# Gate and up of a SwiGLU FFN by seven block products in six of eleven pairs

## The chip, the core and the metric

The kernel runs on one NeuronCore of a Trainium2 chip. The metric is the device time of one execution in microseconds (us). TensorE (PE) multiplies, VectorE (DVE), ScalarE (ACT) and GpSimd (POOL) do the elementwise work, and the queue of SyncE (SP) issues most loads from memory (DMA). Every engine works through its own instruction stream and waits for others at semaphores. Products land in PSUM, eight banks of 128 x 512 float32; all else lies in SBUF.

## What is computed

One layer of a decoder trunk: 512 tokens of width 1024 in float32. A norm, an input projection, a gated-MLP group beside a sparse-attention group, an output projection and a residual; then the part that changes, an FFN of inner width 2816, and a last norm:

```python
h = rmsnorm(x, norm_ffn_w[l])
x = x + (jax.nn.silu(h @ w_gate[l]) * (h @ w_up[l])) @ w_down[l]
return rmsnorm(x, final_norm_w)
```

## The kernel before

Precision is held by splitting. Every operand of a product is split into a high part in fp32r (a copy on ScalarE, `copy_a`, L79) and a low part, the float32 remainder (a subtraction on VectorE, `sub`, L76). `mm3` (L113) then makes three products of one: high by high, high by low, low by high. Products of the trace at L114, L115 and L116 are these three.

The FFN starts behind `ffn_norm`, which turns the normed tokens by transposes (against the tile `ident`) and keeps them as `h2h` and `h2l`, each two tiles of 4 contraction blocks x 512 tokens. The inner width is 22 blocks of 128 columns, in 11 pairs. `gate_up(f)` (L720) loads the gate and the up columns of one block (512 KB each, `load_raw`, L85, three buffers "wr"), splits them into half-weight buffers ("wh", eight of 4 KB a partition) and multiplies: for gate and for up 8 contraction blocks by `mm3`, 512 tokens wide, which is 48 products into two PSUM banks. Block 0 is done in two halves of 256 tokens, because its second half waits for the last norm. `gate_act(f)` (L696) applies SiLU on ScalarE and the multiplication by up on VectorE; after the second block of a pair it also forms four sums of token and width quarters (`ss`) and splits all seven pieces into `ah` and `al`.

`down` (L782) is already a product by seven: it takes a group of pairs (`FFN_GROUPS`: 2, 3, 3 and 3 pairs), loads 1 MB of down weights a pair ("wd", three buffers of their own), and makes seven products M1, M2, M5, M6, M3, M7, M4. For each it splits one quarter or one combination of quarters of every pair's weights (`product`, L789); the combinations are formed in place in the raw buffer (`diffs`, `t2_of`, `t4_of`, L808 to L816), so a raw buffer comes free only when M4's weights have been split. The results are added into the residual `x2` (`accumulate`, L774), mostly twice each.

The program is written in this order: block by block, then the group's `down`, then the next group. The scheduler of the tile framework sets the order within each engine's stream when the program is built: it places what is ready by a timing model of its own, earlier program text first, so splits of later weights stand between earlier work where buffers allow. A tile waits for a free buffer of its tag. Pools that were closed (`first_pools`) leave their place to the pools of the FFN (`weights_f`, `temps_f`, L763), and a new tile waits for the old tiles that lay there.

Of the kernel before, what the change touches and what calls it, by code (L numbers as in the profile page):

```python
# [18 lines left out]
P = 128  # L19
S = 512  # L20
# [11 lines left out]
NG = 24  # L32
FFN_GROUPS = (4, 6, 6, 6)
START = (("S", 0), ("T", 0), ("W", 0), ("K", 0), ("S", 1), ("T", 1), ("W", 1), ("S", 2), ("K", 1), ("T", 2),
         ("W", 2), ("S", 3), ("K", 2), ("T", 3), ("W", 3), ("K", 3))
BANKS = (3, 2, 2, 1)
NBIG, NP, NRAW, NSPL, T4, T2 = 11, 3, 3, 4, 3, 4
NHALF, NDOWN = 8, 3


@with_exitstack
def hybrid_gmlp_nsa_kernel(
# [16 lines left out]
    wp, tp, sp = [p.__enter__() for p in first_pools]  # L59

# [28 lines left out]

    def split(raw, shape, name, eng=None, spare=False, behind=None, halves=False):  # L90
        if spare:
            w = bp.tile([P, 2, *shape], F32R, tag="P", name=f"{name}_s", bufs=NP)
            hi, lo = w[:, 0], w[:, 1]
        elif halves:
            hi = wp.tile([P, *shape], F32R, tag="wh", name=f"{name}_h", bufs=NHALF)
            lo = wp.tile([P, *shape], F32R, tag="wh", name=f"{name}_l", bufs=NHALF)
# [8 lines left out]
    def load_cols(w, r0, nk, c0, n, name, eng=None, spare=False, behind=None, halves=False):  # L105
        src = w[r0:r0 + nk * P, c0:c0 + n].rearrange("(k p) f -> p k f", p=P)
        return split(load_raw(src, [nk, n], name), [nk, n], name, eng, spare, behind, halves)

# [9 lines left out]
    def bcast_row(vec, n, name, tag=None):  # L118
        t = cp.tile([P, DM if tag else n], F32, name=name, tag=tag or name)[:, :n]
        nc.sync.dma_start(t, bass.AP(tensor=vec.tensor, offset=vec.offset, ap=[[0, P], [1, n]]))  # L120
        return t
# [18 lines left out]

    ident = cp.tile([P, P], F32, name="ident")
    make_identity(nc, ident)
    ones = cp.tile([1, P], F32, name="ones")
    nc.vector.memset(ones, 1.0)
# [48 lines left out]
    ps = zp.__enter__()  # L193
    NB = {**dict(zip("MSTO", BANKS)), "G": 2, "A": 2, "B": 2, "C": 2}

# [76 lines left out]
    maskw = cp.tile([P, S], F32, name="maskw")  # L272
# [3 lines left out]
    cmask = cp.tile([P, NT, 32], F32, name="cmask")  # L276
# [3 lines left out]
    valid = cp.tile([P, 1], F32, name="valid")  # L280
    nc.gpsimd.memset(valid, 1.0)
# [4 lines left out]
    nc.tensor.transpose(vps[:, :80], vec, ident[:80, :80])  # L286
    vecT = cp.tile([P, 80], F32, name="vecT")
    copy_a(vecT, vps[:, :80])
# [37 lines left out]

    sel = cp.tile([2 * NX, NX], F32, name="sel")
    done = nc.vector.tensor_tensor(out=sel, in0=ident[:2 * NX, 0:NX], in1=ident[:2 * NX, NX:2 * NX], op=OP.add)
    after(done, kept)
    pair = cp.tile([P, 2, 32], F32, name="pair")  # L330
# [129 lines left out]
    for k in range(4):  # L460
        pt = bank("T", [P, NT, P], f"pta{k}")
        for t in range(NT):
# [223 lines left out]
    acts = []  # L686
    n_act = [0]
    raw_act = [None]

    def act_tile(name):  # L690
        n_act[0] += 1
        if (n_act[0] - 1) % 8 < NP:
            return bp.tile([P, 7, 256], F32R, tag="P", name=name, bufs=NP)
        return b8([P, 7, 256], F32R, name)

    def gate_act(f):  # L696
        pg, e = gu.pop(f)[1], f % 2
        if e == 0:
            raw_act[0] = t4([P, 4, 256], F32, f"sg{f}")
        sg = raw_act[0]  # L700
        own = sg[:, 2 * e:2 * e + 2].rearrange("p a c -> p (a c)")
        nc.scalar.activation(own, pg[0], AF.Silu)
        nc.vector.tensor_tensor(out=own, in0=pg[1], in1=own, op=OP.mult)  # L703
        if e == 0:
            return
        ss = t4([P, 4, 256], F32, f"ss{f}")
        ah, al = act_tile(f"ah{f}"), act_tile(f"al{f}")
# [7 lines left out]
        acts.append((ah, al))  # L715


    gu = {}

    def gate_up(f, part=None):  # L720
        if not part:
            behind = mixed[-1] if f == 0 else last_norm if f == 1 else None
            ws = [load_cols(w, 0, KD, f * P, P, f"w{'gu'[a]}{f}", spare=f == 0, behind=behind, halves=f > 0)
                  for a, w in ((0, w_gate), (1, w_up))]
            gu[f] = ws, [bank("G" if part is None else "S", [P, S], f"gu{f}{a}") for a in range(2)]
        cut = slice(0, S) if part is None else slice(part * 256, part * 256 + 256)
# [55 lines left out]
    def down(gi, pairs):  # L782
        raws = []
        for p in pairs:
            r = wp.tile([P, 2, 2, 512], F32, tag="wd", name=f"wd{p}_r", bufs=NDOWN)
            nc.sync.dma_start(r, w_down[2 * p * P:(2 * p + 2) * P].rearrange("(e p) (h c) -> p e h c", p=P, h=2))
            raws.append(r)

        def product(name, slot, tag, first, src, before=None):  # L789
# [51 lines left out]

    f0 = 0
    onw = None
    for gi, nb in enumerate(FFN_GROUPS):
        acts.clear()
        for f in range(f0, f0 + nb):
            if f > 0:
                gate_up(f)
                gate_act(f)
# [53 lines left out]
```

## Time and profile before

| what | value |
|---|---|
| median of three runs | 619.64 us (615.88 to 620.91) |
| the profiled execution | 617.18 us |
| its span, first to last instruction | 615.4 us |
| granted TensorE clock, mean | 0.998 |
| bytes moved by DMA | 61.33 MB, mean 100 GB/s |

The rows further down name the engine, the line of the kernel, the operation and the tiles it writes and reads, with partitions x elements. On a timeline row the first number is the start from the beginning of the span, the second the duration, both in us; a bracket tells how long the engine stood idle before it and what ended that. Successive instructions of one engine overlap in part, so the distance of two starts is what one costs in a run of them, not its duration.

### The profile page before, as it was taken

Reading aid. Unit: us, or ns where it says so; the run is one execution under the profiler, and the core shown is the slowest. Engines: PE = TensorE matmul, PEld = TensorE weight load, DVE = VectorE, ACT = ScalarE, POOL = GpSimd, SP = SyncE. Lnnn points to the kernel's source line nnn. Section 1 sums busy time; section 2 is a strip of 40 time slices with the busy share of each in tenths; the row PEclk is TensorE's granted clock in tenths of the full one; section 3 lists DMA queues with packets and bytes.
Section 4 is the critical chain, followed back from the end, with each engine's and each line's share of the span. In section 5 each row is a group of like instructions: output and inputs, shape, how many; then the busy total and the mean of one; then the engine's idle time right before and its main releaser. Section 6 shows DMA issues by size and latency. Waiting matters only on the chain.

```text
span 615.4 us, 7662 instructions
## 1 busy us (share of the span) xinstructions
PE 598.2 (97%) x2812; PEld 487.3 (79%) x2812; DVE 400.7 (65%) x729; ACT 297.7 (48%) x547; POOL 68.2 (11%) x113
## 2 busy tenths in 40 slices
PE   8999899998999999999999999999999999999994
PEld 5878778786788777888888888888888888888883
DVE  4752779647898976746694437794437694446696
ACT  6653367649877875434342323442323353233354
POOL 3100100004453473000000000000000000000001
PEclk9999999999999999999999999999999999999999
DMA  8451534534000012089036331037321028320003
GB/s 292 147 143 50 180 114 143 175 123 143 2 2 1 1 36 68 1 240 304 4 98 210 103 103 34 1 138 238 99 87 56 1 96 260 89 68 1 0 2 136
DMA packets 73495, 61.33 MB, mean 100 GB/s; under 512 B 3681, under 2 KB 64113, under 8 KB 73458
## 3 DMA queue, kind: packets, MB, share of 16 engines
q1 hardware_dynamic: 72880, 59.80, 31.4%
q10 hardware_dynamic: 578, 1.05, 0.5%
q8 instruction: 22, 0.36, 0.3%
q14 instruction: 15, 0.12, 0.1%
HBM read 58.74 MB, written 2.10 MB: 99 GB/s over the span
## 4 chain that ended last, share of the span: by engine, by line
PE 87%; DVE 5%; DMA 2%; POOL 2%; ACT 2%; issue 1%; POOLq 0%; SPq 0%; DVEq 0%; ACTq 0%
PE gu L115 13%; PE gu L116 13%; PE gu L114 13%; PE o L652 3%; PE pA L114 3%; PE ptp L632 3%; PE pA L115 3%; PE pA L116 3%; PE s L558 3%; PE po L115 2%; PE po L116 2%; PE po L114 2%; PE pC L114 2%; PE pC L115 2%; PE pC L116 2%
## 5 line engine op out<-in xcount | busy, mean ns | idle before, releaser
L114 PE MATMUL gu<-h2h,wg_h 128*128 128x512 f32 x168 | 65.4, 389 | 0.0
L115 PE MATMUL gu<-h2l,wg_h 128*128 128x512 f32 x168 | 65.4, 389 | 0.0
L116 PE MATMUL gu<-h2h,wg_l 128*128 128x512 f32 x168 | 65.4, 389 | 0.0
L114 PE MATMUL gu<-h2h,wu_h 128*128 128x512 f32 x168 | 65.4, 389 | 0.0
L115 PE MATMUL gu<-h2l,wu_h 128*128 128x512 f32 x168 | 65.4, 389 | 0.0
L116 PE MATMUL gu<-h2h,wu_l 128*128 128x512 f32 x168 | 65.4, 389 | 0.0
L79 ACT ACTIVATE wu_h<-wu_r 128x1024 fp32r<-128x1024 f32 x21 | 22.3, 1061 | 64.9 <-PE gu L115 48.4
L703 DVE TENSOR_TENSOR sg<-gu,sg 128x512 f32<-128x512 f32 x22 | 15.2, 692 | 57.0 <-PE gu L116 57.0
L76 DVE TENSOR_TENSOR wg_l<-wg_r,wg_h 128x1024 fp32r<-128x1024 f32 x21 | 25.7, 1223 | 40.7 <-ACT wg_h L79 40.3
L79 ACT ACTIVATE wg_h<-wg_r 128x1024 fp32r<-128x1024 f32 x21 | 22.3, 1060 | 47.8 <-PE gu L115 40.9
L169 POOL TENSOR_TENSOR rstd_y<-s_y,mhalf 128x1 f32<-128x1 f32 x4 | 3.0, 754 | 345.9 <-DVE s_y L166 341.1
L563 ACT ACTIVATE P<-P,nm 128x128 f32<-128x128 f32 (+3 forms) x64 | 35.5, 559 | 5.4 <-DVE nm L561 5.1
L82 POOL TENSOR_SCALAR P<-P,sm 128x128 f32<-128x128 f32 (+3 forms) x64 | 34.1, 556 | 32.2 <-DVE sm L570 15.0
L116 PEld LDWEIGHTS gu<-h2h,wu_l 128*128 128x128 f32 x168 | 31.6, 188 | 6.6
L116 PEld LDWEIGHTS gu<-h2h,wg_l 128*128 128x128 f32 x168 | 31.5, 187 | 6.6
L114 PEld LDWEIGHTS gu<-h2h,wg_h 128*128 128x128 f32 x168 | 31.6, 188 | 6.5
L115 PEld LDWEIGHTS gu<-h2l,wu_h 128*128 128x128 f32 x168 | 31.5, 188 | 6.6
L115 PEld LDWEIGHTS gu<-h2l,wg_h 128*128 128x128 f32 x168 | 31.5, 188 | 6.5
L114 PEld LDWEIGHTS gu<-h2h,wu_h 128*128 128x128 f32 x168 | 31.5, 188 | 6.5
L561 DVE CUSTOM_DVE_ANT_0 P<-s,maskw 128x128 f32<-128x128 f32 (+3 forms) x64 | 29.5, 481 | 4.5 <-PE s L558 4.0
L652 PE MATMUL o<-PT,Vt 128*128 128x512 f32 x80 | 31.1, 439 | 0.2
L76 DVE TENSOR_TENSOR PT<-ptp,PT 128x512 fp32r<-128x512 f32 x40 | 26.6, 684 | 5.7 <-ACT PT L79 5.5
(510 smaller groups left out, 1501.6 us busy)
## 6 DMA issues: line engine op xcount, KB each, us to landing
wg_r<-in_w_gate_dram SPq DMA_DIRECT2D x22, 512.0 KB, 4.7
wu_r<-in_w_up_dram SPq DMA_DIRECT2D x22, 512.0 KB, 3.9
wd_r<-in_w_down_dram SPq DMA_DIRECT2D x11, 1024.0 KB, 4.8
wo_r<-in_w_o_dram SPq DMA_DIRECT2D x8, 512.0 KB, 4.8
x_sb<-in_x_dram SPq DMA_DIRECT2D x4, 512.0 KB, 8.3
wv_r<-in_w_in_dram SPq DMA_DIRECT2D x4, 512.0 KB, 6.7
wu_r<-in_w_in_dram SPq DMA_DIRECT2D x4, 512.0 KB, 5.0
w1k_r<-in_cmp_k_w_dram SPq DMA_DIRECT2D x4, 512.0 KB, 4.3
```

The lines of the kernel that those rows point to most:

```text
L76: return (eng or nc.vector).tensor_tensor(out=o, in0=a, in1=hi.bitcast(F32), op=OP.subtract)
L79: return nc.scalar.activation(o, a, AF.Copy)
L82: nc.gpsimd.tensor_scalar(out=o, in0=a, scalar1=s, scalar2=1.0, op0=OP.mult, op1=OP.mult)
L114: nc.tensor.matmul(ps, lhsT=sh, rhs=mh, start=first, stop=False, skip_group_check=more)
L115: nc.tensor.matmul(ps, lhsT=sh, rhs=ml, start=False, stop=False, skip_group_check=more)
L116: nc.tensor.matmul(ps, lhsT=sl, rhs=mh, start=False, stop=last, skip_group_check=more)
L558: nc.tensor.matmul(sb, lhsT=q, rhs=KAB[kv][:, a, b0:b0 + nbr, :n], start=(a == 0), stop=(a == 1))
L561: nc.vector.tensor_tensor_reduce(out=pr, in0=sb[:, br], in1=maskw[:, S - n:], scale=-0.125, scalar=BIG, op0=OP.add, op1=OP.min, accum_out= ...
L563: e = nc.scalar.activation(pr, pr, AF.Exp, bias=nm[b], scale=-1.0, accum_out=sm[b])
L632: nc.tensor.transpose(pt[:, hh], src, ident)
L652: nc.tensor.matmul(of, lhsT=Vt[:, b0 + br, j, kv], rhs=PTs[u][:, a], start=(first and a == 0), stop=False)
L703: nc.vector.tensor_tensor(out=own, in0=pg[1], in1=own, op=OP.mult)
```

## The change

For the pairs 2, 3, 5, 6, 8 and 9 gate and up are computed together as a 2 x 2 block product by seven products in place of eight: the rows of the result are gate and up, the contraction is halved, the tokens are halved. So the products are 256 tokens wide, and weights and tokens are combined beforehand: the token combinations once (`token_sums`), the weight combinations in each pair, in place. The other pairs are done plainly but loaded and split by pair. The sums of the seven products are finished on VectorE and ScalarE in the buffers `sg` and `ss`.

The raw buffers are pooled anew: one tag "wr" of three 1 MB buffers serves gate, up and down loads. The constants of the first part (`ident` among them) move from the lasting pool to one of the pools that are closed before the FFN, ahead of the others there. PSUM has six banks of one tag and two for "B". The activations `ah`, `al` lie in named places (`ACT_HOMES`), with two buffers "xa" in the weights pool. The diff, cut:

```diff
-FFN_GROUPS = (4, 6, 6, 6)
+FFN_GROUPS = (2, 3, 3, 3)
+SEVEN = (2, 3, 5, 6, 8, 9)
+ACT_HOMES = (("xa", "xa", "b8", "P"), ("P", "P", "P", "b8", "xa", "xa"))
...
-NHALF, NDOWN = 8, 3
+NHALF, NPAIR, NXA = 8, 3, 2
...
-    first_pools = [tc.tile_pool(name="weights", bufs=2), tc.tile_pool(name="temps", bufs=3),
+    first_pools = [tc.tile_pool(name="consts_a", bufs=1), tc.tile_pool(name="weights", bufs=2), tc.tile_pool(name="temps", bufs=3),
...
-    ident = cp.tile([P, P], F32, name="ident")
+    ident = kp.tile([P, P], F32, name="ident")
...
-    NB = {**dict(zip("MSTO", BANKS)), "G": 2, "A": 2, "B": 2, "C": 2}
+    NB = {**dict(zip("MSTO", BANKS)), "G": 6, "B": 2}
...
+    def keep_acts(p, sg, ss):
+        ah, al = act_tile(f"ah{p}"), act_tile(f"al{p}")
         copy_a(ah[:, 0:3], sg[:, 1:4])
...
+        elif part is None:
+            raw = wp.tile([P, 2, KD, P], F32, tag="wr", name=f"wgu{f}_r", bufs=NPAIR)
+            ws = []
+            for a, w in ((0, w_gate), (1, w_up)):
+                nc.sync.dma_start(raw[:, a], w[:, f * P:(f + 1) * P].rearrange("(k p) f -> p k f", p=P))
+                ws.append(halves(raw[:, a], [KD, P], f"w{'gu'[a]}{f}", last_norm))
...
+    def halves(src, shape, name, behind=None):
+        hi, lo = [wp.tile([P, *shape], F32R, tag="wh", name=f"{name}_{c}", bufs=NHALF) for c in "hl"]
+        for step in (copy_a(hi, src), sub(lo, src, hi)):
...
+    def pair_raw(p):
+        raws = []
+        for c, w in (("g", w_gate), ("u", w_up)):
+            r = wp.tile([P, KD, 256], F32, tag="wr", name=f"w{c}{p}_r", bufs=NPAIR)
+            nc.sync.dma_start(r, w[:, p * 256:(p + 1) * 256].rearrange("(k p) f -> p k f", p=P))
+            raws.append(r)
+        return raws
+
+    def plain_pair(p):
+        sg, ss = t4([P, 4, 256], F32, f"sg{p}"), t4([P, 4, 256], F32, f"ss{p}")
+        z = {}
+        for a, r in enumerate(pair_raw(p)):
+            for kh in range(2):
+                hi, lo = halves(r[:, 4 * kh:4 * kh + 4], [4, 256], f"w{'gu'[a]}{p}{kh}")
+                for e in range(2):
+                    if kh == 0:
+                        z[e, a] = bank("G", [P, S], f"gu{p}{a}{e}")
+                    for k in range(4):
+                        c = slice(e * P, (e + 1) * P)
+                        mm3(z[e, a], hi[:, k, c], lo[:, k, c], h2h[kh][:, k], h2l[kh][:, k],
+                            kh + k == 0, kh == 1 and k == 3)
+        for e in range(2):
+            gate_act(sg, e, (z[e, 0], z[e, 1]))
+        keep_acts(p, sg, ss)
...
+    def token_sums():
+        rs = []
+        for a in range(2):
+            r = bp.tile([P, 2, 4, 256], F32, tag="P", name=f"tok{a}", bufs=NP)
+            for c in range(2):
+                cut = slice(c * 256, c * 256 + 256)
+                nc.vector.tensor_tensor(out=r[:, c], in0=h2h[a][:, :, cut].bitcast(F32),
+                                        in1=h2l[a][:, :, cut].bitcast(F32), op=OP.add)
+            rs.append(r)
+        y11, y12, y21, y22 = rs[0][:, 0], rs[0][:, 1], rs[1][:, 0], rs[1][:, 1]
+        for o, x, y in ((y11, y12, y11), (y12, y22, y12), (y22, y22, y11), (y21, y21, y22)):
+            nc.vector.tensor_tensor(out=o, in0=x, in1=y, op=OP.subtract)
+        for a in range(2):
+            hi, lo = b8([P, 2, 4, 256], F32R, f"th{a}"), b8([P, 2, 4, 256], F32R, f"tl{a}")
+            for c in range(2):
+                copy_a(hi[:, c], rs[a][:, c])
+                sub(lo[:, c], rs[a][:, c], hi[:, c])
...
+    def seven_pair(p):
+        sg, ss = t4([P, 4, 256], F32, f"sg{p}"), t4([P, 4, 256], F32, f"ss{p}")
+        sgv = sg.rearrange("p (e a) c -> p e a c", a=2)
+        gate, late, up2 = sgv[:, :, 0], sgv[:, :, 1], ss[:, 0:2]
+        rg, ru = pair_raw(p)
+        a11, a12, a21, a22 = rg[:, 0:4], rg[:, 4:8], ru[:, 0:4], ru[:, 4:8]
...
+            for e in range(2):
+                c = slice(e * P, (e + 1) * P)
+                for k in range(4):
+                    mm3(z[tag][:, e], w[0][:, k, c], w[1][:, k, c], y[0][:, k], y[1][:, k],
+                        first and e + k == 0, k == 3, not first or e > 0)
...
+        w = unit(1, a11)
+        vec2(a11, a11, a21, OP.subtract)
+        vec2(a21, a21, a22, OP.add)
+        product(1, "A", w, y11)
+        copy_a(gate, z["A"])
+        w = unit(5, a21)
+        vec2(a21, a22, a11, OP.subtract)
+        product(5, "C", w, t1)
+        copy_a(up2, z["C"])
+        product(6, "A", unit(6, a21), t2n)
+        copy_a(late, z["A"])
+        w = unit(2, a12)
+        vec2(a12, a12, a21, OP.subtract)
+        product(2, "B", w, y21)
+        vec2(gate, z["B"], gate, OP.add)
+        nc.scalar.activation(gate, gate, AF.Silu)
+        product(7, "A", unit(7, a11), t3)
+        vec2(up2, z["A"], up2, OP.add)
+        product(3, "C", unit(3, a12), y22)
+        vec2(late, z["C"], late, OP.add)
+        nc.scalar.activation(late, late, AF.Silu)
+        product(4, "A", unit(4, a22), t4n)
+        vec2(gate, z["A"], gate, OP.mult)
+        vec2(late, up2, late, OP.mult)
+        keep_acts(p, sg, ss)
...
-            r = wp.tile([P, 2, 2, 512], F32, tag="wd", name=f"wd{p}_r", bufs=NDOWN)
+            r = wp.tile([P, 2, 2, 512], F32, tag="wr", name=f"wd{p}_r", bufs=NPAIR)
...
+        for p in range(p0, p0 + n):
+            if p == 0:
+                gate_act(sg0, 1, gate_up(1))
+                keep_acts(0, sg0, ss0)
+            elif p in SEVEN:
+                seven_pair(p)
+            else:
+                plain_pair(p)
+        if gi == 0:
+            token_sums()
```

## Rows read from the trace of the kernel before

**Rows 1.** The page, part 1: busy time, share of the span, instructions
```profile
PE 598.2 (97%) x2812; PEld 487.3 (79%) x2812; DVE 400.7 (65%) x729; ACT 297.7 (48%) x547; POOL 68.2 (11%) x113
```

**Rows 2.** Busy time by engine in four stretches of the FFN
```profile
core 0: us, PE busy (x) PEld busy (x) DVE busy (x) ACT busy (x) POOL busy (x), PEclk, DMA share, GB/s
273.00:283.90 10.90, 10.90 (x51) 9.04 (x50) 5.84 (x6) 4.74 (x6) 0.00 (x0) 1.00 0.96 308
283.90:305.75 21.85, 21.85 (x98) 18.07 (x97) 14.77 (x21) 7.33 (x12) 0.00 (x0) 1.00 0.39 126
305.75:325.70 19.95, 19.95 (x88) 16.25 (x87) 18.89 (x28) 9.93 (x14) 0.00 (x0) 1.00 0.37 127
390.30:419.10 28.80, 28.80 (x127) 23.57 (x126) 26.88 (x41) 14.42 (x21) 0.00 (x0) 1.00 0.32 107
```

**Rows 3.** Timeline of PE: start us, duration us, line, what it computes
```profile
270.20 0.28 PE L116 MATMUL gu<-h2h,wg_s 128*128 128x256 f32 x1
...
273.08 0.40 PE L114 MATMUL gu<-h2h,wg_h 128*128 128x512 f32 x1
...
283.99 0.39 PE L114 MATMUL gu<-h2h,wg_h 128*128 128x512 f32 x1
...
305.75 0.39 PE L114 MATMUL pA<-wd0M,ah 128*128 128x512 f32 x1
```

**Rows 4.** Timeline of DVE around 310 us
```profile
308.10 0.42 DVE L711 TENSOR_TENSOR ss<-ss,sg 128x256 f32<-128x256 f32 x1
308.43 0.95 DVE L76 TENSOR_TENSOR al<-sg,ah 128x768 fp32r<-128x768 f32 x1
309.30 0.42 DVE L711 TENSOR_TENSOR ss<-sg,ss 128x256 f32<-128x256 f32 x1
309.63 0.68 DVE L76 TENSOR_TENSOR wd0M<-wd_r,wd0M 128x512 fp32r<-128x512 f32 x1
310.24 0.68 DVE L776 TENSOR_TENSOR x<-pA,x 128x512 f32<-128x512 f32 x1
310.84 1.22 DVE L76 TENSOR_TENSOR al<-ss,ah 128x1024 fp32r<-128x1024 f32 x1
311.99 0.68 DVE L776 TENSOR_TENSOR x<-pA,x 128x512 f32<-128x512 f32 x1
```

**Rows 5.** Timeline of ACT, same stretch
```profile
309.75 1.06 ACT L79 ACTIVATE ah<-ss 128x1024 fp32r<-128x1024 f32 x1 [1.62 <-DVE ss L711]
310.72 0.61 ACT L79 ACTIVATE wd1M<-wd_r 128x512 fp32r<-128x512 f32 x1
```

**Rows 6.** Timeline of SP's queue, then PE, at the second down group
```profile
408.38 3.01 SPq L786 DMA_DIRECT2D wd_r<-in_w_down_dram  x2
...
411.03 0.37 SPq L786 DMA_DIRECT2D wd_r<-in_w_down_dram  x1
...
390.31 0.39 PE L114 MATMUL pA<-wd2M,ah 128*128 128x512 f32 x1
...
419.10 0.39 PE L114 MATMUL gu<-h2h,wg_h 128*128 128x512 f32 x1
```

**Rows 7.** The page, part 6: DMA issues of 1 MB, count, KB each, us to landing
```profile
wd_r<-in_w_down_dram SPq DMA_DIRECT2D x11, 1024.0 KB, 4.8
```

**Rows 8.** Timeline of all engines at the start of the FFN
```profile
264.01 0.38 SPq L87 DMA_DIRECT2D wg_r<-in_w_gate_dram  x1
...
265.10 3.33 SPq L87 DMA_DIRECT2D wg_r<-in_w_gate_dram  x1
...
265.47 1.04 PE L180 MATMUL pt_f<-ident,xf 128*128 128x128 f32 x8
...
270.27 1.06 ACT L79 ACTIVATE wg_h<-wg_r 128x1024 fp32r<-128x1024 f32 x1 [3.08 <-DMA wg_r<-in_w_gate_dram]
```

**Rows 9.** Waits in 300 to 600 us: total us, times, longest
```profile
engine line waited for: us in total, times, longest us
DVE sg L703 <- PE gu L116: 54.5, 19, 3.4
```

More of the change, by code (lines that the diff above doesn't have):

```diff
@@ L56, in hybrid_gmlp_nsa_kernel @@
     bp = ctx.enter_context(tc.tile_pool(name="big", bufs=NBIG))
-    first_pools = [tc.tile_pool(name="weights", bufs=2), tc.tile_pool(name="temps", bufs=3),
+    first_pools = [tc.tile_pool(name="consts_a", bufs=1), tc.tile_pool(name="weights", bufs=2), tc.tile_pool(name="temps", bufs=3),
                    tc.tile_pool(name="small", bufs=4)]
-    wp, tp, sp = [p.__enter__() for p in first_pools]
+    kp, wp, tp, sp = [p.__enter__() for p in first_pools]
     def b8(shape, dt, name):
@@ L88, in load_raw, with split @@
         return raw
-    def split(raw, shape, name, eng=None, spare=False, behind=None, halves=False):
+    def split(raw, shape, name, eng=None, spare=False, behind=None):
         if spare:
@@ L103, in split, with load_cols @@
         return hi, lo
-    def load_cols(w, r0, nk, c0, n, name, eng=None, spare=False, behind=None, halves=False):
+    def load_cols(w, r0, nk, c0, n, name, eng=None, spare=False, behind=None):
         src = w[r0:r0 + nk * P, c0:c0 + n].rearrange("(k p) f -> p k f", p=P)
-        return split(load_raw(src, [nk, n], name), [nk, n], name, eng, spare, behind, halves)
+        return split(load_raw(src, [nk, n], name), [nk, n], name, eng, spare, behind)
     def after(later, earlier):
@@ L118, in bcast_row @@
     def bcast_row(vec, n, name, tag=None):
-        t = cp.tile([P, DM if tag else n], F32, name=name, tag=tag or name)[:, :n]
+        t = (cp if tag else kp).tile([P, DM if tag else n], F32, name=name, tag=tag or name)[:, :n]
         nc.sync.dma_start(t, bass.AP(tensor=vec.tensor, offset=vec.offset, ap=[[0, P], [1, n]]))
@@ L286, in hybrid_gmlp_nsa_kernel @@
     nc.tensor.transpose(vps[:, :80], vec, ident[:80, :80])
-    vecT = cp.tile([P, 80], F32, name="vecT")
+    vecT = kp.tile([P, 80], F32, name="vecT")
     copy_a(vecT, vps[:, :80])
@@ L324, in blocks @@
         sub(X2[nm][:, :, 1, :], xff, X2[nm][:, :, 0, :])
-    sel = cp.tile([2 * NX, NX], F32, name="sel")
+    sel = kp.tile([2 * NX, NX], F32, name="sel")
     done = nc.vector.tensor_tensor(out=sel, in0=ident[:2 * NX, 0:NX], in1=ident[:2 * NX, NX:2 * NX], op=OP.add)
     after(done, kept)
-    pair = cp.tile([P, 2, 32], F32, name="pair")
+    pair = kp.tile([P, 2, 32], F32, name="pair")
     idv = ident.rearrange("p (a e n) -> p a e n", a=2, e=2)
@@ L686, in hybrid_gmlp_nsa_kernel @@
     acts = []
-    n_act = [0]
-    raw_act = [None]
+    homes = []
     def act_tile(name):
[L691 to L707, printed above, removed]
+        tag = homes.pop(0)
+        if tag == "b8":
+            return b8([P, 7, 256], F32R, name)
+        pool, n = (bp, NP) if tag == "P" else (wp, NXA)
+        return pool.tile([P, 7, 256], F32R, tag=tag, name=name, bufs=n)
+    def keep_acts(p, sg, ss):
+        ah, al = act_tile(f"ah{p}"), act_tile(f"al{p}")
         copy_a(ah[:, 0:3], sg[:, 1:4])
@@ L715, in gate_act @@
         acts.append((ah, al))
+    def gate_act(sg, e, pg):
+        own = sg[:, 2 * e:2 * e + 2].rearrange("p a c -> p (a c)")
+        nc.scalar.activation(own, pg[0], AF.Silu)
+        nc.vector.tensor_tensor(out=own, in0=pg[1], in1=own, op=OP.mult)
     gu = {}
     def gate_up(f, part=None):
-        if not part:
-            behind = mixed[-1] if f == 0 else last_norm if f == 1 else None
-            ws = [load_cols(w, 0, KD, f * P, P, f"w{'gu'[a]}{f}", spare=f == 0, behind=behind, halves=f > 0)
+        if part == 0:
+            ws = [load_cols(w, 0, KD, f * P, P, f"w{'gu'[a]}{f}", spare=True, behind=mixed[-1])
                   for a, w in ((0, w_gate), (1, w_up))]
-            gu[f] = ws, [bank("G" if part is None else "S", [P, S], f"gu{f}{a}") for a in range(2)]
+            gu[f] = ws, [bank("S", [P, S], f"gu{f}{a}") for a in range(2)]
+        elif part is None:
[4 more added lines that the diff above has]
+                ws.append(halves(raw[:, a], [KD, P], f"w{'gu'[a]}{f}", last_norm))
+            gu[f] = ws, [bank("G", [P, S], f"gu{f}{a}") for a in range(2)]
         cut = slice(0, S) if part is None else slice(part * 256, part * 256 + 256)
@@ L730, in gate_up @@
                     k == 0, k == KD - 1)
+        return gu[f][1]
+    def halves(src, shape, name, behind=None):
+        hi, lo = [wp.tile([P, *shape], F32R, tag="wh", name=f"{name}_{c}", bufs=NHALF) for c in "hl"]
+        for step in (copy_a(hi, src), sub(lo, src, hi)):
+            if behind is not None:
+                after(step, behind)
+        return hi, lo
+    def pair_raw(p):
[5 more added lines that the diff above has]
+        return raws
@@ new lines, in hybrid_gmlp_nsa_kernel @@
+    TH, TL = [], []
+    def token_sums():
[15 more added lines that the diff above has]
+                sub(lo[:, c], rs[a][:, c], hi[:, c])
+            TH.append(hi)
+            TL.append(lo)
@@ new lines, in seven_pair, with vec2, product, unit @@
+    def seven_pair(p):
[4 more added lines that the diff above has]
+        a11, a12, a21, a22 = rg[:, 0:4], rg[:, 4:8], ru[:, 0:4], ru[:, 4:8]
+        t1, t3, t4n, t2n = [(TH[a][:, c], TL[a][:, c]) for a in range(2) for c in range(2)]
+        y11, y21, y22 = [(h2h[a][:, :, c], h2l[a][:, :, c])
+                         for a, c in ((0, slice(0, 256)), (1, slice(0, 256)), (1, slice(256, 512)))]
+        z = {}
+        def vec2(o, x, y, op):
+            nc.vector.tensor_tensor(out=o, in0=x, in1=y, op=op)
+        def product(n, tag, w, y):
+            first = tag not in z
+            if first:
+                z[tag] = bank("G", [P, 2, 256], f"g{tag}{p}")
+            for e in range(2):
[3 more added lines that the diff above has]
+                        first and e + k == 0, k == 3, not first or e > 0)
+        def unit(n, src):
+            return halves(src, [4, 256], f"w{p}M{n}")
+        w = unit(1, a11)
[23 more added lines that the diff above has]
+        keep_acts(p, sg, ss)
@@ L800, in product @@
                 if first:
-                    banks[tag, c] = bank(tag, [P, 512], f"p{tag}{gi}{c}")
+                    banks[tag, c] = bank("B" if tag == "B" else "G", [P, 512], f"p{tag}{gi}{c}")
                 z, ts = banks[tag, c], slice(c * P, (c + 1) * P)
@@ L840, in down @@
             add(0, 0, "A")
-    f0 = 0
+    p0 = 0
     onw = None
-    for gi, nb in enumerate(FFN_GROUPS):
+    for gi, n in enumerate(FFN_GROUPS):
         acts.clear()
[L846 to L849, printed above, removed]
+        homes[:] = ACT_HOMES[min(gi, 1)]
+        for p in range(p0, p0 + n):
[8 more added lines that the diff above has]
+            token_sums()
         if gi == len(FFN_GROUPS) - 1:
             onw = bcast_row(final_norm_w, DM, "onw", tag="wb")
-        down(gi, range(f0 // 2, (f0 + nb) // 2))
-        f0 += nb
+        down(gi, range(p0, p0 + n))
+        p0 += n
     def finish(t, order):
```

28 lines of the change are left out of this document (13 added, 15 removed).

## The prediction

> **What bounds the kernel now.** I read the page's table of engines first: TensorE is busy 97% of the span, VectorE 65%, ScalarE 48% [rows 1]. [...] So from 273 us to the end of the products the time is the number of products times their spacing, and VectorE, which splits every weight into a high and a low part, is next in line. Then the timeline of PE for that spacing, since a product's own duration (0.28 or 0.39 us) overlaps with its neighbours: 24 products of 256 columns start between 270.20 and 273.08 us, 0.120 us each; the 96 of 512 columns of one pair take 283.99 to 305.75 us, 21.76 us or 0.2267 us each [rows 3]. Half the columns cost 53%, not 50%.
>
> **TensorE.** A plain pair is 2 blocks x 2 matrices x 8 contraction tiles x 3 terms = 96 products of 512 columns: 21.76 us. A pair by seven products is 7 x 2 blocks x 4 tiles x 3 terms = 168 products of 256 columns: 168 x 0.120 = 20.16 us. Gain 1.60 us a pair, 9.6 us in six pairs. The eighth of the columns that is saved would be 2.72 us; the spacing takes back 1.12 us. Break-even is a spacing of 0.1295 us. The down products keep their number.
>
> **VectorE.** The start-to-start times in an unbroken run are 0.33 us for 256 columns, 0.87 for 768, 0.6 for 512 (from PSUM too) and 1.15 for 1024 [rows 4]. One pair's activations (keep_acts) cost 4 x 0.33 + 0.87 + 1.15 = 3.3 us in either form. Plain: 4 low parts of 1024 (4.6), 2 multiplies (1.2), 3.3: 9.1 us under 21.76 us of TensorE. Seven: 7 low parts (8.05), 4 in-place weight sums (4.6), 3 additions and 2 multiplies of 512 (3.0), 3.3: 19.0 us under 20.16 us. It fits with 1.2 us to spare; against the old 21.76 us, with 2.8. Over a group of seven, seven, plain and down, VectorE needs 2 x 19.0 + 9.1 + 26.9 = 74 us of TensorE's 2 x 20.16 + 21.76 + 28.8 = 91 us. So its throughput suffices, if the slack of the plain pair can be carried over: the eight half-weight buffers let it run four units ahead, about 11 us. ScalarE: 0.97 us a 1024 [rows 5], seven of them, 1.8 us of activations, five pieces of 0.6 from PSUM or to SiLU: some 12 us of 20. It doesn't bind.
>
> **What is lost again, term by term.**
>
> *Start of the FFN.* Today the first gate load is issued at 264.01 us and its conversion starts at 270.27, so the products follow on at 273.08 without a gap [rows 3, 8]. In the change the FFN's weight pool begins where the new pool consts_a lay, whose identity is read by the transposes that end at 266.5 us [rows 8]. If the first raw buffer lies over it, everything is 2.5 us late: conversion 272.8, high part 273.8, the low part 1.15 us after that and wanted two products in: 0.7 to 1.4 us. Nothing if it lies elsewhere; if one of the 1 MB loads of pair 1 goes ahead, 3.4 us more at the 308 GB/s of that stretch [rows 2]. I take 1.0 (0 to 4).
>
> *Token sums.* 8 sums and 4 low parts of 1024 columns: 12 x 1.15 = 13.8 us of VectorE, 3.9 of ScalarE. They need only the normed tokens, so they can go anywhere from 273 to 305.75 us, where VectorE has 32.75 - 5.84 - 14.77 = 12.1 us free [rows 2]. 1.7 us stick out and push the first down group's conversions. I take 0.5 (0 to 1.7; all 13.8 if they were issued in a block ahead of the down conversions, and the cover were gone).
>
> *Three raw buffers for all.* Loads of gate, up and down now share three buffers of 1 MB, and a down group of three pairs holds all of them until its last product's conversions. Today these free the first at 408.38 and the second at 411.03 us, with the down group's products ending at 419.10 us: 10.7 and 8.1 us ahead [rows 6]. A 1 MB load lands 4.8 us after its issue [rows 7], two in a row some 3.4 us apart [rows 2]: gate weights 5.9 us ahead of the end, up weights between 3.3 and 2.5 ahead. The first product's weights are then ready in time. The second needs two sums (2.3) and a high part (0.97) after the up weights: 0.0 to 0.8 us after the end, wanted at 2.88. The third needs low part, sum, high and low part more (1.15 + 1.15 + 0.97 + 1.15): 4.4 us on, ready at 4.4 to 5.2, wanted at 2 x 2.88 + 0.24 = 6.0. Between them stand up to four additions of the down group (0.6 each). So up to 1.6 us late; 0.5 at each of three boundaries, 1.5 in all (0 to 5).
>
> *Order inside a pair.* 0.25 us for each seven-product pair, 1.5 us in all (0 to 6): with 1.2 us to spare, an operation that waits for TensorE in VectorE's queue holds the conversions behind it. The trace of before shows such waits, 19 of 2.9 us on average between 300 and 600 us [rows 9]; there they cost nothing because VectorE had time.
>
> Sum: 9.6 - 1.0 - 0.5 - 1.5 - 1.5 = 5.1 us. The profiled execution took 617.18 us (span 615.4 and 1.8 around it), which gives 612.1; the median of the runs shown is 619.64, 2.5 above it, which gives 614.5. I state 613.3, between the two.
>
> **The rivals.** *The full gain.* The scheduler places the new work so that TensorE never waits: 9.6 us less at most, 607.6 in the profiled execution's terms. For it: TensorE has no gap anywhere in the FFN today, although down groups load VectorE to 93% [rows 2]. Against it: margins of a microsecond at three boundaries.
>
> *VectorE becomes the bound, slower than before.* The place is the seven-product pair, where four operations on VectorE wait for a product's end (the gate, up and late additions and the multiply). If two of them stand 2.9 us each [rows 9] with conversions behind them, VectorE takes 19.0 + 5.7 = 24.7 us a pair, 3.0 over the plain pair: six pairs, 18 us, 635 us. It decides from 2.8 us of such waiting in a pair. Against it: in the down stretches VectorE works through the same mixture at 26.88 of 28.80 us [rows 2]. [...]
>
> *The raw buffers eat the gain.* If the down conversions end 4 us later than today, the up weights come 1.6 us after the down group's end: the second product starts at 1.6 + 2.3 + 0.97 = 4.9 in place of 2.9, the third 1.2 later still: 3.2 us a boundary, 9.6 in three: 617. For it: nothing else can take a fourth buffer. Against it: the 10.7 us of [rows 6].
>
> *The change doesn't do what it says:* products of 256 columns spaced at 0.135 us: 168 x 0.135 = 22.7 us, 0.9 over, 5.5 us slower, 623. Against it speaks the same kind of product on the same operands at 0.120 [rows 3].
>
> **How the numbers follow.** About 1% (6.2 us) is what a measurement of this kernel can tell from no change. Chances: my sum 0.45, with its own range of 2 to 8 us gained (611.6 to 617.6 by the median; 0.13 of it past 1%, 0.32 within); full gain 0.30, all past 1%; raw buffers 0.13 (0.11 within, 0.02 slower); VectorE bound 0.09 (0.08 slower); spacing 0.03 (slower). Faster 0.43, no change 0.44, slower 0.13. The range: the full gain off the lowest run shown, 615.9 - 9.6 = 606, to 622, where gain and 2 us more are lost; VectorE's bound lies outside.
>
> **What would show it.** Right: in the timeline of PE, 168 products of 256 columns at 0.120 us in each of six pairs, 20.2 us; VectorE over 90% busy there; token sums between 273 and 306 us; gaps of PE of about a microsecond, at the first block after the start and behind each down group, ended by a conversion or a load. Wrong: gaps inside the seven-product pairs ended by VectorE (then it is the bound), waits for the load of up weights of several us, or a first gate conversion well past 273 us.

## The result and the profile after

The changed kernel takes 627.33 us in the median of four runs (626.75 to 627.99), beside 618.38 us for the kernel before on the same chip. The ratio is 1.0145, 95% interval 1.0097 to 1.0193: slower by 9 us, outside the stated range. The profiled execution has a span of 625.0 us. Its table of engines, to be held against [rows 1]:

```profile
PE 597.8 (96%) x3244; PEld 503.6 (81%) x3244; DVE 473.0 (76%) x801; ACT 329.2 (53%) x587; POOL 68.3 (11%) x113
```

TensorE is busy as long as before, 597.8 against 598.2 us, though the change takes out columns, and it stands idle 10 us more in the longer span (27.2 us against 17.2). VectorE has 72 us more to do. Where the time went shows only by stretches. From the timeline of PE I took the start of each stage, once for either kernel (in us; the pairs before are two blocks each, 65.28 us for three pairs, so 21.76 for one):

| stage | before | after |
|---|---|---|
| first 512-column product of the FFN starts at | 273.08 | 273.26 |
| block 1 and pair 1 | 32.67 | 32.67 |
| first down group, then pair 2 | 19.96 + 21.08 | 30.38 + 24.47 |
| pairs 3, 5, 6, 8, 9, together | 108.8 | 104.05 |
| pairs 4, 7, 10, each | 21.76 | 21.79, 21.78, 21.79 |
| the other down groups | 28.79, 28.86, 28.95 | 28.89, 28.87, 29.02 |

(Pair 2's 21.08 is 21.76 less three products that the scheduler had put into the down group.) So the loss has one place: the first down group and pair 2, 54.85 us in place of 41.04. Busy time in that place, then in pair 3 and in the second down group, with the columns of [rows 2]:

```profile
core 0: us, PE busy (x) PEld busy (x) DVE busy (x) ACT busy (x) POOL busy (x), PEclk, DMA share, GB/s
305.93:336.31 30.38, 23.50 (x87) 17.30 (x86) 29.95 (x38) 11.60 (x15) 0.00 (x0) 0.83 0.11 36
336.31:360.78 24.47, 21.86 (x168) 21.45 (x166) 19.45 (x18) 10.96 (x13) 0.00 (x0) 0.93 0.41 129
360.78:380.93 20.15, 20.15 (x170) 20.15 (x169) 18.58 (x23) 12.46 (x15) 0.00 (x0) 1.00 0.37 133
402.72:431.61 28.89, 28.89 (x128) 23.58 (x127) 26.43 (x41) 11.96 (x18) 0.00 (x0) 1.00 0.35 109
```

The reader is to see three things. Pair 3 is what was forecast: 168 products in 20.15 us at a granted clock of 1.00. The second down group is as before. But in the first down group VectorE is busy for 29.95 of 30.38 us while TensorE is at 23.50, and the mean granted clock is 0.83. What VectorE did there is in its timeline:

```profile
301.17 0.69 DVE L78 TENSOR_TENSOR wd0M<-wd_r,wd0M 128x512 fp32r<-128x512 f32 x1 [3.73 <-ACT wd0M L81]
...
308.61 0.95 DVE L78 TENSOR_TENSOR al<-sg,ah 128x768 fp32r<-128x768 f32 x1
309.48 0.42 DVE L700 TENSOR_TENSOR ss<-sg,ss 128x256 f32<-128x256 f32 x1
309.81 2.35 DVE L776 TENSOR_TENSOR tok<-h2h,h2l 128x1024 f32<-128x1024 f32 x2
312.08 1.22 DVE L78 TENSOR_TENSOR al<-ss,ah 128x1024 fp32r<-128x1024 f32 x1
313.22 2.35 DVE L776 TENSOR_TENSOR tok<-h2h,h2l 128x1024 f32<-128x1024 f32 x2
315.49 1.22 DVE L781 TENSOR_TENSOR tok<-tok 128x1024 f32<-128x1024 f32 x1
316.62 0.68 DVE L890 TENSOR_TENSOR x<-pA,x 128x512 f32<-128x512 f32 x1
...
321.76 1.22 DVE L781 TENSOR_TENSOR tok<-tok 128x1024 f32<-128x1024 f32 x1
322.90 0.68 DVE L890 TENSOR_TENSOR x<-pA,x 128x512 f32<-128x512 f32 x1
```

The token sums (`tok`, `tl`) do not stand in the free time between 273 and 306 us, where VectorE waits 3.7 us in one piece. They begin at 309.81, right behind the first write of pair 1's `al` (308.61), and hold the queue until 325.8 us; the additions into `x` stand among them, at 316.62 and 322.90. TensorE waits for exactly these two. M1 writes two PSUM banks pA, one for each half of its tokens, and its last products there end by 310.5 us. Each addition reads one of the banks, and M6 accumulates into the same banks, so the six products of a bank stand behind its addition:

```profile
309.85 0.63 PE L115 MATMUL pA<-wd1M,al 128*128 128x512 f32 x2
...
317.36 0.50 PE L113 MATMUL pA<-wd0M,ah 128*128 128x512 f32 x1 [2.81 <-DVE x L890]
...
318.99 0.63 PE L115 MATMUL pA<-wd1M,al 128*128 128x512 f32 x1
323.63 0.79 PE L113 MATMUL pA<-wd0M,ah 128*128 128x512 f32 x1 [4.02 <-DVE x L890]
324.23 0.63 PE L114 MATMUL pA<-wd0M,ah 128*128 128x512 f32 x1
324.65 0.63 PE L115 MATMUL pA<-wd0M,al 128*128 128x512 f32 x1
```

The first wait is 2.81 us, the second 4.02, and the products behind the second come 0.42 us apart where 0.2267 is normal. The granted clock by two-microsecond pieces says why:

```profile
core 0: us, PE busy (x) PEld busy (x) DVE busy (x) ACT busy (x) POOL busy (x), PEclk, DMA share, GB/s
...
316.00:318.00 2.00, 0.64 (x3) 0.56 (x4) 2.00 (x3) 1.06 (x1) 0.00 (x0) 1.00 0.00 0
318.00:320.00 2.00, 1.61 (x5) 0.75 (x3) 2.00 (x3) 1.06 (x1) 0.00 (x0) 0.54 0.00 0
320.00:322.00 2.00, 0.00 (x0) 0.00 (x0) 2.00 (x3) 1.06 (x1) 0.00 (x0) 0.50 0.00 0
...
326.00:328.00 2.00, 2.00 (x7) 1.33 (x5) 2.00 (x4) 0.42 (x1) 0.00 (x0) 0.50 0.00 0
328.00:330.00 2.00, 1.94 (x8) 1.16 (x7) 2.00 (x5) 0.00 (x0) 0.00 (x0) 0.90 0.00 0
```

After the first wait the clock falls from 1.00 to 0.50 and stays there until about 328 us. Of the 10.4 us that the group takes more than before, 6.8 are the two waits; the rest is the slower products, which keep TensorE busy for 23.50 us and not 19.95 [rows 2].

So two additions of 0.68 us, which had their products by 310.5 us, stood behind sums of 1.2 us that nobody needs before pair 2's second product (340.95 us). In VectorE's timeline the sums ahead of them end at 316.71 and 322.98 us, and the additions start at 316.62 and 322.90.

Pair 2 then waits for its up weights. SP's queue, with the first gate load of the FFN as its first row:

```profile
266.70 0.37 SPq L724 DMA_DIRECT2D wgu_r<-in_w_gate_dram  x1
...
286.75 0.37 SPq L746 DMA_DIRECT2D wg_r<-in_w_gate_dram  x1
331.93 0.37 SPq L746 DMA_DIRECT2D wu_r<-in_w_up_dram  x1
```

Pair 2's gate load goes out at 286.75, its up load only at 331.93 us, when the late down conversions give a raw buffer back. TensorE waits for what is made of it, in pair 2's second product (M5):

```profile
340.95 0.39 PE L113 MATMUL gC<-th,w2M_h 128*128 128x256 f32 x1 [1.85 <-ACT w2M_h L81]
...
342.21 0.58 PE L115 MATMUL gC<-th,w2M_l 128*128 128x256 f32 x1 [0.76 <-DVE w2M_l L78]
```

These 2.6 us, and the clock that falls once more behind them (0.50 from 343 to 345 us, a mean of 0.93 over the pair), are what pair 2 takes over 20.16 us.

### The profile page after: what moved, and what is told of

The parts are those of the page before. It is cut to its first block, busy times and chain, and to the rows that moved or that the text cites. A ratio compares the mean times of both kernels' runs of the same rounds, so it can differ in the third digit from the quotient of the medians.

```text
span 625.0 us, 8610 instructions
## 1 busy us (share of the span) xinstructions
PE 597.8 (96%) x3244; PEld 503.6 (81%) x3244; DVE 473.0 (76%) x801; ACT 329.2 (53%) x587; POOL 68.3 (11%) x113
## 4 chain that ended last, share of the span: by engine, by line
PE 67%; DVE 19%; DMA 6%; ACT 4%; POOL 2%; issue 2%; POOLq 0%; ACTq 0%; SPq 0%; DVEq 0%
PE gu L114 6%; PE gu L115 6%; PE gu L113 6%; PE o L651 3%; PE ptp L631 3%; PE s L557 3%; DVE x L890 2%; PE po L115 2%; PE po L114 2%; PE gA L115 2%; PE po L113 2%; PE gA L113 2%; PE gA L114 2%; DMA wu_r<-in_w_up_dram 2%; DVE wu_r L804 2%
## 5 line engine op out<-in xcount | busy, mean ns | idle before, releaser
L113 PE MATMUL gu<-h2h,wg_h 128*128 128x512 f32 x72 | 28.1, 390 | 0.0
L114 PE MATMUL gu<-h2l,wg_h 128*128 128x512 f32 x72 | 28.1, 390 | 0.0
L115 PE MATMUL gu<-h2h,wu_l 128*128 128x512 f32 x72 | 28.0, 389 | 0.0
L115 PE MATMUL gu<-h2h,wg_l 128*128 128x512 f32 x72 | 28.0, 389 | 0.0
L113 PE MATMUL gu<-h2h,wu_h 128*128 128x512 f32 x72 | 28.0, 389 | 0.0
L114 PE MATMUL gu<-h2l,wu_h 128*128 128x512 f32 x72 | 28.0, 389 | 0.0
L631 PE MATMUL ptp<-ident,P 128*128 128x128 f32 x160 | 25.7, 275 | 2.0 <-POOL P L84 1.9
L81 ACT ACTIVATE PT<-ptp 128x512 fp32r<-128x512 f32 x40 | 22.6, 593 | 8.5 <-PE ptp L631 8.1
L557 PE MATMUL s<-KAB,QS 128*128 128x512 f32 (+2 forms) x96 | 27.0, 374 | 0.0
L890 DVE TENSOR_TENSOR x<-pA,x 128x512 f32<-128x512 f32 x32 | 21.8, 685 | 1.9 <-PE pA L115 1.9
```

The lines of the kernel that those rows point to most:

```text
L81: return nc.scalar.activation(o, a, AF.Copy)
L113: nc.tensor.matmul(ps, lhsT=sh, rhs=mh, start=first, stop=False, skip_group_check=more)
L114: nc.tensor.matmul(ps, lhsT=sh, rhs=ml, start=False, stop=False, skip_group_check=more)
L115: nc.tensor.matmul(ps, lhsT=sl, rhs=mh, start=False, stop=last, skip_group_check=more)
L557: nc.tensor.matmul(sb, lhsT=q, rhs=KAB[kv][:, a, b0:b0 + nbr, :n], start=(a == 0), stop=(a == 1))
L631: nc.tensor.transpose(pt[:, hh], src, ident)
```

## The experiments

All ratios are to the kernel before, run beside it on the same chip. In the single profiles the first 512-column product of the FFN starts anywhere from 273.1 to 275.4 us. The difference is there long before the FFN: at the TensorE instruction that the kernel after starts at 161 us, the version with early sums is 0.57 us behind that kernel and the one without sums 2.18; at that product it is 0.55 and 2.12. So beside each time I give the FFN stretch, from that product to the last product's start: 334.16 us before, 343.48 us after.

**The other homes.** The token sums' buffers have the tags P and b8. In the change, pair 1's `ah` and `al` take one buffer of each, and they are asked for ahead of the sums.

```diff
-ACT_HOMES = (("xa", "xa", "b8", "P"), ("P", "P", "P", "b8", "xa", "xa"))
+ACT_HOMES = (("b8", "P", "xa", "xa"), ("P", "P", "P", "b8", "xa", "xa"))
```

> Edit: in group 0 the activations of pair 0 lie in b8 and P, those of pair 1 in xa, so the token sums' buffers (tags P and b8) no longer come after pair 1's in the order of requests. Theory A (the token sums stand late, behind pair 1's activations, only because buffers of a tag are given out in program order; then they hold VectorE ahead of the first down group's splits): the sums run between 273 and 306 us and the loss of 11 us in the first down group goes: 614 to 618 us. Theory B (VectorE has no room for 13.8 us anywhere in group 0): the stall only moves, 624 to 628. Theory C (the late load of pair 2's up weights is the loss): 624 to 628 as well, since the loads stay.

Measured: 620.97 us, ratio 1.0067 (1.0042 to 1.0092); FFN stretch 336.58. VectorE's timeline of this kernel:

```profile
288.49 0.95 DVE L78 TENSOR_TENSOR al<-sg,ah 128x768 fp32r<-128x768 f32 x1
...
289.69 2.35 DVE L776 TENSOR_TENSOR tok<-h2h,h2l 128x1024 f32<-128x1024 f32 x2
```

The sums moved 20 us forward with no change to their place in the program, and start again 1.2 us behind the first write of an `al` in tag P, this time pair 0's. That is Theory A's cause. The time lies between A's forecast and that of the others: 6.9 us of the stretch are recovered, but the free time before 289 us is still missed, and the first down splits stand among and behind the sums, so group and pair 2 still take 22.79 + 24.91 us.

**The call moved ahead of pair 1.**

```diff
                 keep_acts(0, sg0, ss0)
+                token_sums()
...
-        if gi == 0:
-            token_sums()
```

> Edit: the call of token_sums moves from behind pair 1 to ahead of it, so it also comes ahead of pair 1's splits in priority. Theory A: 613 to 618 us, as with the other homes or a little less. Theory B: pair 1's splits come late instead, a stall of 5 to 12 us near 284 to 300 us, 622 to 628. Theory C: 624 to 628.

Measured: 614.36 us, ratio 0.9957 (0.9943 to 0.9971); FFN stretch 330.65. The first sum now stands here:

```profile
255.63 1.22 DVE L776 TENSOR_TENSOR tok<-h2h,h2l 128x1024 f32<-128x1024 f32 x1
```

No activation in tag P or b8 is asked for ahead of the sums here. Five of the eight sums start before the first 512-column product (273.81 us), some of them while the norm still runs; the prediction's window from 273 us left that time out. The first down group takes 20.14 us and pair 2 20.43. Theory B falls: the same 13.8 us of sums fit in without a stall when they come early. So does C as the main cause. The kernel is faster than before, by 2.8 us; six pairs still take 126.04 us together, where 6 x 20.16 = 120.96 was worked out.

**No token sums** (left out, as the expectation says).

> Leaves out the token sums: the seven products take the plain token halves where combinations belong. Theory A and B: all that the token sums cost is gone, 611 to 614 us (the lost 11 us of the first down group and some of the 4 us in pair 2). Theory C: the up load of pair 2 still waits for the first down buffer, over 618.

Measured: 615.68 us, ratio 0.9978 (0.9966 to 0.9990); FFN stretch 331.05. No better than with the sums placed early, and the six pairs lose as much as there. So early sums cost nothing, and the rest of the loss is something else. The 611 to 614 of A and B counted only the sums.

**No pair by seven products** (`SEVEN = ()`, no sums).

> No pair by seven products and no token sums; the loads by pair and the new pools stay. If pools and loads cost nothing: 618 to 620 us, as the kernel before. If the three shared raw buffers stall the group boundaries by themselves (Theory C): 622 or more. With the third kernel of this call it also gives the gain of six pairs by seven products: 9.6 us by the product spacing less what the pairs lose inside.

Measured: 618.21 us, ratio 1.0015 (1.0003 to 1.0027); FFN stretch 334.42. The shared raw buffers, the loads by pair and the new pools cost at most 2 us by themselves, 0.3 in the stretch.

What is left in the early version shows in pair 6. SP issues its up load, VectorE stands until it lands, and the chain of sums and splits behind it comes late; the three timelines in this order:

```profile
430.39 0.37 SPq L746 DMA_DIRECT2D wu_r<-in_w_up_dram  x1
```

```profile
436.43 1.23 DVE L804 TENSOR_TENSOR wg_r<-wg_r,wu_r 128x1024 f32<-128x1024 f32 x1 [1.68 <-DMA wu_r<-in_w_up_dram]
...
440.18 1.23 DVE L78 TENSOR_TENSOR w6M_l<-wu_r,w6M_h 128x1024 fp32r<-128x1024 f32 x1 [0.66 <-ACT w6M_h L81]
441.32 0.68 DVE L804 TENSOR_TENSOR sg<-gA,sg 128x512 f32<-128x512 f32 x1
...
442.52 1.22 DVE L804 TENSOR_TENSOR wu_r<-wu_r,wg_r 128x1024 f32<-128x1024 f32 x1
...
445.87 1.22 DVE L78 TENSOR_TENSOR w6M_l<-wu_r,w6M_h 128x1024 fp32r<-128x1024 f32 x1
```

```profile
445.45 0.39 PE L113 MATMUL gA<-th,w6M_h 128*128 128x256 f32 x1
...
446.39 0.38 PE L113 MATMUL gB<-h2h,w6M_h 128*128 128x256 f32 x1 [0.44 <-ACT w6M_h L81]
447.14 0.39 PE L115 MATMUL gA<-th,w6M_l 128*128 128x256 f32 x1 [0.36 <-DVE w6M_l L78]
```

The load goes out at 430.39, when the previous pair's gate buffer is given back after its sixth split, and VectorE can start the first sum at 436.43: 6.0 us. From there M5's low part stands at 440.18, but pair 5's last multiplies (441.32 and on) and its activations follow first, and M6's low part is written from 445.87 to 447.1. TensorE wants it at about 445.7 and continues at 447.14. Two theories: the load (L), or too little throughput of VectorE (V).

**M2 ahead of M5.**

```diff
         product(1, "A", w, y11)
         copy_a(gate, z["A"])
+        product(2, "B", unit(2, a12), y21)
+        vec2(gate, z["B"], gate, OP.add)
+        nc.scalar.activation(gate, gate, AF.Silu)
         w = unit(5, a21)
         vec2(a21, a22, a11, OP.subtract)
         product(5, "C", w, t1)
         copy_a(up2, z["C"])
-        product(6, "A", unit(6, a21), t2n)
+        w = unit(6, a21)
+        vec2(a12, a12, a21, OP.subtract)
+        product(6, "A", w, t2n)
         copy_a(late, z["A"])
...
```

> The early token sums (e2_early, 614.4 us) with the second product moved up: M1, M2, M5, M6, M7, M3, M4. M2's weights need no sum, so the two sums that wait for the up load get one product (2.9 us) more of cover. Theory L (what the seven-product pairs still lose, 0.85 us each over 20.16, is the chain up load, sum, split, sum, split of M5 and M6): 609 to 611 us. Theory V (VectorE has too little throughput in the pair): 613 to 615, since its work is the same.

Measured: 613.74 us, ratio 0.9917 (0.9886 to 0.9949); FFN stretch 329.47, 1.2 less than without. A miss for L as I had put it: pairs 2 and 3 gain (20.03 and 20.39), pairs 6 and 9 don't (21.93 and 21.40). A product's time of cover is not what is missing.

**Six raw buffers of 512 KB.**

```diff
-NHALF, NPAIR, NXA = 8, 3, 2
+NHALF, NPAIR, NXA = 8, 6, 2
...
-        rg, ru = pair_raw(p)
-        a11, a12, a21, a22 = rg[:, 0:4], rg[:, 4:8], ru[:, 0:4], ru[:, 4:8]
+        a11, a21, a22, a12 = [half_raw(p, a, kh) for a, kh in HALF_ORDER]
...
-            r = wp.tile([P, 2, 2, 512], F32, tag="wr", name=f"wd{p}_r", bufs=NPAIR)
+            r = []
+            for e in range(2):
+                r.append(wp.tile([P, 2, 512], F32, tag="wr", name=f"wd{p}{e}_r", bufs=NPAIR))
...
```

with `HALF_ORDER = ((0, 0), (1, 0), (1, 1), (0, 1))`: gate first half, up first half, up second half, gate second half.

> The early token sums with six raw buffers of 512 KB in place of three of 1 MB, the same room: every quarter of a pair's weights and every half of a pair's down weights has its own load and comes free by itself. Theory L: the up quarters land several us earlier, 610 to 612 us. If the chain of VectorE operations behind the load is what counts and not the load: 613 to 615, as Theory V. The smaller loads cost no more than 0.5 us.

Measured: 609.11 us, ratio 0.9836 (0.9800 to 0.9872); FFN stretch 324.97. This version is faster than both kernels. Busy time of its first down group, pairs 2, 3 and 6:

```profile
core 0: us, PE busy (x) PEld busy (x) DVE busy (x) ACT busy (x) POOL busy (x), PEclk, DMA share, GB/s
306.61:326.56 19.95, 19.95 (x91) 16.29 (x90) 19.03 (x29) 8.42 (x12) 0.00 (x0) 1.00 0.34 105
326.56:346.11 19.55, 19.55 (x165) 19.55 (x163) 17.49 (x18) 9.91 (x12) 0.00 (x0) 1.00 0.34 109
346.11:366.27 20.16, 20.16 (x171) 20.16 (x169) 18.00 (x21) 12.44 (x15) 0.00 (x0) 1.00 0.45 156
437.30:457.46 20.16, 20.16 (x170) 20.16 (x169) 18.74 (x23) 12.33 (x15) 0.00 (x0) 1.00 0.46 153
```

TensorE has no gap left: 20.16 us for pair 3 and pair 6, as worked out from the spacing, at a granted clock of 1.00, with VectorE at 18.00 and 18.74 us of it. Theory V falls for six pairs: VectorE's work is the same as in the early version (two half sums in `diffs` for one apart). Theory L holds: SP issues pair 6's first up quarter at 409.87 us, where the whole up load went out at 430.39. A quarter's buffer comes back as soon as that quarter is used up; but the run changes the size of the loads and the order of the quarters with it, and which of the three counts how much is not shown.

**Both edits.** In this kernel the loads were asked for in another order than they are named, so that three of the quarters (a12, a21, a22) are exchanged and the FFN computes something else. Instructions and sizes are as described, but by their use the quarters still come in the order a11, a21, a22, a12: the quarter of M2, now the second product, is asked for last.

> Both edits together, the quarters loaded in the order a11, a12, a21, a22. Theory L: next to no wait of TensorE left in the six pairs, 608 to 610 us: 617.1 less 9.6 and up to 1. Theory V: 613 to 615.

Measured: 610.52 us, ratio 0.9856 (0.9816 to 0.9897); FFN stretch 326.37. No wait of TensorE is listed, but each pair from 3 on takes 20.42 or 20.43 us: 0.27 are lost where M7 begins (451.16 us in pair 6). What causes that was not tried. The run is no test of the order that its expectation names.

**No weight sums** (left out, as the expectation says).

> Leaves out the four weight sums of each seven-product pair (products take the plain quarters), with the early token sums: takes 4.6 us of 19.0 off VectorE in each pair and the wait for the up load off the second product. Theory L and V both: 608 to 610 us; a time of 612 or more would say that TensorE's own spacing, not its feeding, holds the pairs at 21 us.

Measured: 608.94 us, ratio 0.9837 (0.9798 to 0.9876); FFN stretch 324.74; every pair 20.15 or 20.16 us. Both theories had this. It shows that 0.120 us a product is all that the pairs need once they are fed, and that the six small buffers reach the same time with all sums kept.

**Six small buffers with the sums left late.** The kernel after with the edit of the raw buffers alone.

> The kernel after with the six raw buffers of 512 KB alone; the token sums stay where the change put them. If the late token sums and the late up loads are two separate losses: the first down group still takes some 30 us (10 to 11 lost), the pairs 3 to 9 take 20.2 us each and pair 2 at most 21: 617 to 620 us. If the raw buffers were the cause of the first down group's stall as well: 609 to 612, as with both edits.

Measured: 624.42 us, ratio 1.0118 (1.0088 to 1.0148); FFN stretch 339.95. Pairs 3 to 9 by seven products take 20.15 or 20.16 us, but the first down group takes 30.40 and pair 2 24.32. So the stall of the first down group isn't the buffers'. The time lies above the forecast, most of it since pair 2 recovers nothing: its raw buffers still come from the late down splits. Against the six-buffer version with early sums, the late sums cost 339.95 - 324.97 = 15.0 us.

**Nine pairs by seven products** (`SEVEN = (2, 3, 4, 5, 6, 7, 8, 9, 10)`, early sums, six small buffers).

> The early token sums, the six small raw buffers, and all nine pairs from 2 to 10 by seven products, so that no plain pair lends VectorE time ahead of a down group: VectorE needs 3 x 19.0 + 26.9 = 84 us of TensorE's 3 x 20.16 + 28.8 = 89 in a group. If that is enough: three times 1.6 us more gain, 604 to 606 us. If VectorE becomes the bound once its slack is 6% and not 18%: gaps in the down groups or at their start, 607 to 613.

Measured: 610.91 us, ratio 0.9893 (0.9870 to 0.9916); FFN stretch 325.11, no better than with six pairs and inside the 607 to 613 forecast for VectorE as the bound. Busy time of pair 4 and the second down group, and TensorE's waits in the FFN:

```profile
core 0: us, PE busy (x) PEld busy (x) DVE busy (x) ACT busy (x) POOL busy (x), PEclk, DMA share, GB/s
366.52:386.68 20.16, 20.16 (x171) 20.16 (x170) 18.95 (x26) 12.82 (x18) 0.00 (x0) 1.00 0.31 105
386.68:417.52 30.84, 29.37 (x129) 23.37 (x127) 29.13 (x47) 11.69 (x18) 0.00 (x0) 1.00 0.29 91
```

```profile
engine line waited for: us in total, times, longest us
PE pA L113 <- ACT ah L81: 1.7, 3, 0.9
PE pA L113 <- DVE x L889: 0.9, 2, 0.6
```

Pair 4 by seven products is 20.16 us, so 1.6 are gained in each of three groups, 4.8 in all. They are given back behind it: down groups of 30.84, 29.84 and 29.97 us, and 0.6 in each of pairs 5 and 8. VectorE is busy 18.95 of 20.16 and then 29.13 of 30.84 us, and TensorE waits for activations (`ah`) and additions that VectorE feeds. That fits a plain pair that lends VectorE its time ahead of each down group, but it isn't the whole cause. At the second group's late addition VectorE was not short of time:

```profile
413.45 1.23 DVE L78 TENSOR_TENSOR w5M_l<-wg_r,w5M_h 128x1024 fp32r<-128x1024 f32 x1 [1.31 <-ACT w5M_h L81]
414.59 0.68 DVE L889 TENSOR_TENSOR x<-pA,x 128x512 f32<-128x512 f32 x1
```

The addition's last product ends by 412.7 us. VectorE stands idle 1.31 us for pair 5's first split, whose load went out at 408.00 us, and the addition waits behind that split; M4's second bank waits for the addition until 415.33 us. How much either cause takes was not tried apart.

## Why the prediction was wrong, step by step

*TensorE's gain: right.* 168 products of 256 columns at 0.120 us [rows 3] are 20.16 us a pair, measured 20.15 to 20.16 wherever the pair is fed. With both losses mended the FFN stretch is 9.2 us shorter than before, beside 9.6 forecast.

*VectorE's work: right.* 19.0 us a pair were worked out [rows 4]; with nine such pairs 18.95 of 20.16 us are measured. ScalarE's 12 us are 12.82 there. That the slack of the plain pair is needed fits the nine-pair kernel, but is not shown by it alone, since VectorE stands 1.31 us behind a late load there too, with an addition behind it.

*Token sums: the step that failed.* "They need only the normed tokens, so they can go anywhere from 273 to 305.75 us": the data allow it, the buffers don't. The kernels with other homes and with the call moved show that the sums start right behind the first write of the last activation tile of their tag that is asked for before them: 309.81 us here, 289.69 with the other homes, 255.63, with the norm still running, where there is none. I took 0.5 us, had 1.7 as the end of the range, and put "all 13.8 if they were issued in a block ahead of the down conversions" into a bracket without giving it a chance or a place in the range. That is what happened: the late sums cost 12.8 us of this kernel's stretch (343.48 - 330.65) and 15.0 with six small buffers, the block, the late up load behind it and the fallen clock together. This alone turns the 5.1 us that the sum gained into a loss. With the 5.7 us that the raw buffers cost, 12.8 + 5.7 - 9.6 = 8.9 us, where the stretch is 9.3 longer than before.

*Three raw buffers: mechanism right, place and size off.* I priced the up load at the three boundaries, 1.5 us in all, and the order inside a pair at 1.5. With early sums the six pairs lose 126.04 - 120.96 = 5.1 us, and six small buffers take all of it away (5.7 in the stretch: five of pair 2's products, 0.6 us, stand in the down group ahead of it). At the boundaries the price was near: in the kernel after, pairs 5 and 8 lose 0.6 each, where 0.5 was taken. But it isn't only there: with early sums, pair 6, behind pair 5, loses 1.5, pair 3 loses 1.0. My sum of the chain left out that a buffer of 1 MB is held until the sixth of seven splits of the pair ahead, that the up load takes 6.0 us there and not the 4.8 us of a down load [rows 7], and that the previous pair's activations stand between M5's and M6's low parts. Sum of both terms: 3.0 forecast, 5.1 measured; in the kernel after itself, pairs 3, 5, 6, 8 and 9 lose 104.05 - 100.8 = 3.3.

*Start: right in its cause, too dear.* The first gate load goes out at 266.70 us, behind the transposes that read `ident`, and not at 264.01 [rows 8]. But it is used 4.2 us after its issue and not 6.3:

```profile
270.94 1.06 ACT L81 ACTIVATE wg_h<-wgu_r 128x1024 fp32r<-128x1024 f32 x1 [3.59 <-DMA wgu_r<-in_w_gate_dram]
```

The conversion starts at 270.94, 0.7 us later than before and not 2.5, and the products follow at 273.26: 0.2 us late, not 1.0, and without a wait of TensorE ahead of them. The load ahead of it in the queue (`onw`) was issued 0.5 us earlier before and 3.0 us earlier after; that this is the reason was not tried.

*The rivals.* Slower came, with 0.13, but not by the rival that I priced: VectorE's queue was the mechanism, in one block of the first down group, not in the pairs. The raw-buffer rival was worth 5 us, not 9.6. The full gain is what the mended kernel shows.

## What to carry to other kernels

Work that "can go anywhere" by its data goes where its buffers are given out: before costing a block at nothing, look which tiles of the same tag are asked for ahead of it in the program, and when those are first written. The price of a misplaced block is what stands behind it on its engine, here two additions of 0.68 us on VectorE, for which TensorE waited 2.81 and 4.02 us. Where one buffer holds parts that are used up at different times, split it and its load; with the order of the loads changed along with it, it cost nothing here and gave 5.7 us.

## What the runs showed of the hardware

Behind the wait of 2.81 us in the first down group the granted clock fell from 1.00 (316 to 318 us) to 0.50, and it came back only at some 328 us, behind the second wait, of 4.02 us, though TensorE was at work again from 323.63; at 0.50 the products of 512 columns came 0.42 us apart, where 0.2267 is normal. Loads of 512 KB in place of 1 MB, twice as many, showed no cost: the kernel with six small buffers loads the same weights, takes 609.11 us, and no wait of its TensorE in the FFN is listed.
